# The opening of a hybrid encoder layer on one core: every engine's order written out, and the input projection fed with normed rows only

## Chip, core and metric

The kernel runs on one core of a Trainium2 chip. Time is the device time of one execution, in microseconds (us); smaller is better. TensorE (PE) multiplies, ScalarE (ACT) and VectorE (DVE) work elementwise, GpSimd (POOL) fills and adds, SyncE (SP) issues most loads. Weights of a product are loaded in a row of their own (PEld).

## What is computed

One layer over 528 rows (16 meta tokens and 512 inputs) of width 1024. The rows are normed, one wide projection feeds a recurrent head group (RWKV-7), an attention head group with a forget gate (FoX) and two gates; their results are merged and projected, and an MLP follows.

```python
u = rmsnorm(h, norm_mix[l])
proj = u @ w_in[l]
feat_rw = proj[..., :C_RW]
feat_fx = proj[..., C_RW:C_RW + C_FX]
gates = jax.nn.sigmoid((proj[..., C_RW + C_FX:] + b_gate[l]).astype(jnp.float32))
...
h = h + (merged @ w_o[l]).astype(h.dtype)
z = rmsnorm(h, norm_mlp[l])
h = h + (jnp.square(jax.nn.relu(z @ w_up[l])) @ w_down[l]).astype(h.dtype)
```

The time shift `f + mu * (token_shift(f) - f)` is laid on the RWKV features; `log_f = log_sigmoid(fl + b_f)`, summed up along the rows, gives the forget rows F of the eight attention heads.

## The kernel before

All operands stand transposed: 128 features of a block on the partitions, rows along the free side, in two halves of 264 rows (t = 0, 1). A float32 operand is split into a rounded part and a remainder (`hi`, `lo`), and a product of two such operands is three fast products (`passes`). The rows are split into `uhi` and `ulo`, eight blocks of 128 features each, in four chunks of two; each block of 128 output features of `w_in` is 24 products per half (8 blocks, 3 passes). Plain float32 products take two passes, each at half the pace.

The opening, before the loops over heads, does this. The input comes in four chunks per half (`xt`). For each half, ScalarE squares a chunk (L352), rounds it times the norm's gain to `uhi` (L355), VectorE makes the remainder `ulo` (L356): rows that are **not yet scaled** by the inverse root. TensorE sums the squares with a matrix of ones (L360, `pss`), makes the forget gate's eight columns from the raw rows (L365, `pf`, 24 products per half), and ScalarE takes the inverse root with a logarithm and an exponential (L368, L369, `rs`). The first two blocks of `w_in` (LORA and GD, the low-rank inputs of the decay and of the output gate) are projected from the raw rows in `proj` (L304), and their results are rescaled by `rs` in `normed_shift` (L377) before the time shift (L317, L318). Behind them the forget rows are finished (L381 to L388), and `xt` is scaled, rounded and split anew (L398, L400, L401), which overwrites `uhi` and `ulo` with normed rows for all other blocks.

From there a planner (`Turns`, with the estimate `Clock`) decides while the program is written in which order streams go on: projections of further blocks (L501, with weights rounded at L470 and L471), the first head pair's decay (L733 to L743) and keys (L750 to L769), its score products (L804), attention. A block's weights arrive in two halves (`wraw`, four buffers, one load each on SyncE). Inside the opening a scheduler that follows dependences and readiness orders the engines' queues; every engine then executes its queue in order.

Results of a projection lie in banks: two with the tag `pj`, and one each with `ch` and `py` that the opening may use too. A bank is free again when the time shift has read it.

## Time and profile before

| | us |
|---|---|
| median of 3 runs | 848.71 (846.68 to 849.0) |
| the profiled execution | 847.68 |
| its span, first to last instruction | 845.9 |
| TensorE busy | 827.1 |
| VectorE busy | 615.0 |
| ScalarE busy | 460.4 |
| GpSimd busy | 115.7 |

The profile is one execution. A group of instructions is told by line, engine, operation and tile, with its count, its busy time and the mean of one; the time that an engine stood before an instruction is in brackets, with what released it. The end of a product is modelled, so that products overlap in the rows: the pace is read from the starts.

### The profile page before, as it was taken

The page shows a single profiled execution, that of the slowest core. Times are in us where ns is not written, and L with a number is a line of the kernel's source. Part 1 is how long each engine was busy: PE and PEld are TensorE (multiplying, and loading weights), DVE is VectorE, ACT ScalarE, POOL GpSimd, SP SyncE. Part 2 cuts the span into 40 slices and gives each one's busy share as a digit, 9 for nine tenths or more (in the row PEclk, how much of TensorE's full clock was granted, in tenths as well). Part 3 has the DMA queues.
Part 4 walks back from the last instruction along what each step waited for, and adds up shares of the span by engine and source line. Part 5 has one row for each costly group of instructions (what it writes and reads, how often), then busy time and mean ns, then how long its engine had stood idle before and what let it go on. Part 6 is the DMA issues. An engine that isn't in the chain of part 4 may idle for free.

```text
span 845.9 us, 15282 instructions
## 1 busy us (share of the span) xinstructions
PE 827.1 (98%) x5740; PEld 679.4 (80%) x5740; DVE 615.0 (73%) x1226; ACT 460.4 (54%) x947; POOL 115.7 (14%) x121
## 2 busy tenths in 40 slices
PE   7899999999999999999999999999999999999998
PEld 6888976878988777787688779888888888888886
DVE  7996986589879757566456564876777777767688
ACT  7767537774765276554555452664355435544452
POOL 1010200001000000000022002204700550055000
PEclk9999999999999999999999999999999999999999
DMA  6132131201213222123487422642743374246321
GB/s 229 59 103 66 65 101 42 77 27 64 63 59 95 87 76 77 39 87 101 151 264 228 149 81 88 208 141 56 256 137 100 95 240 128 86 137 200 110 91 74
DMA packets 51338, 95.88 MB, mean 113 GB/s; under 512 B 5816, under 2 KB 6968, under 8 KB 51264
## 3 DMA queue, kind: packets, MB, share of 16 engines
q1 hardware_dynamic: 47680, 86.52, 32.4%
q0 software_dynamic: 1280, 4.20, 1.6%
q10 hardware_dynamic: 2304, 4.20, 1.4%
q8 instruction: 45, 0.74, 0.4%
q14 instruction: 29, 0.24, 0.1%
HBM read 88.57 MB, written 6.31 MB: 112 GB/s over the span
## 4 chain that ended last, share of the span: by engine, by line
PE 76%; DVE 8%; ACT 4%; DMA 4%; issue 2%; POOL 1%; SPq 0%; DVEq 0%; ACTq 0%; POOLq 0%
PE pj L501 21%; PE po L1149 21%; PE po L1267 12%; PE pd L1267 5%; PE po L1119 2%; PE pw L857 2%; DMA gl<-gd 2%; PE psc L611 1%; PE py L656 1%; DMA wraw<-in_wo 1%; PE ppt L640 1%; DVE wlo L236 1%; PE pch L923 1%; PE psr L804 1%; DMA wraw<-in_wup 1%
## 5 line engine op out<-in xcount | busy, mean ns | idle before, releaser
L501 PE MATMUL pj<-uhi,whi 128*128 128x264 f32 (+1 forms) x480 | 166.0, 346 | 0.0
L501 PE MATMUL pj<-ulo,whi 128*128 128x264 f32 (+1 forms) x480 | 154.1, 321 | 1.2 <-DVE ulo L401 1.2
L501 PE MATMUL pj<-uhi,wlo 128*128 128x264 f32 (+1 forms) x480 | 154.0, 321 | 0.0
L501 PEld LDWEIGHTS pj<-uhi,whi 128*128 128x128 f32 x480 | 90.3, 188 | 14.6 <-issue 6.6
L236 DVE TENSOR_TENSOR wlo<-wraw,whi 128x512 fp32r<-128x512 f32 x88 | 67.1, 771 | 46.9 <-ACT whi L235 46.9
L501 PEld LDWEIGHTS pj<-ulo,whi 128*128 128x128 f32 x480 | 90.5, 188 | 8.1 <-issue 1.7
L501 PEld LDWEIGHTS pj<-uhi,wlo 128*128 128x128 f32 x480 | 90.3, 188 | 7.0
L1149 PE MATMUL po<-zhi,whi 128*128 128x512 f32 (+1 forms) x248 | 94.8, 382 | 0.0
L1149 PE MATMUL po<-zlo,whi 128*128 128x512 f32 (+1 forms) x248 | 94.8, 382 | 0.0
L1149 PE MATMUL po<-zhi,wlo 128*128 128x512 f32 (+1 forms) x248 | 94.8, 382 | 0.0
L235 ACT CAST whi<-wraw 128x512 fp32r<-128x512 f32 x88 | 54.0, 618 | 51.9 <-DMA wraw<-in_wup 21.5
L470 ACT CAST whi<-wraw 128x512 fp32r<-128x512 f32 x80 | 48.8, 616 | 38.8 <-PE pj L501 37.9
L471 DVE TENSOR_TENSOR wlo<-wraw,whi 128x512 fp32r<-128x512 f32 x80 | 57.2, 723 | 13.1 <-ACT whi L470 11.3
L270 ACT CAST whi<-t 128x512 fp32r<-128x512 f32 x64 | 39.9, 624 | 44.5 <-DVE wlo L271 20.6
L271 DVE TENSOR_TENSOR wlo<-t,whi 128x512 fp32r<-128x512 f32 x64 | 49.4, 784 | 18.9 <-ACT whi L270 18.0
L1267 PE MATMUL po<-wlo,fhi 128*128 128x512 f32 x160 | 62.7, 392 | 0.2 <-DVE wlo L271 0.2
L1267 PE MATMUL po<-whi,flo 128*128 128x512 f32 x160 | 62.3, 389 | 0.0
L1267 PE MATMUL po<-whi,fhi 128*128 128x512 f32 x160 | 61.9, 389 | 0.0
L1195 POOL TENSOR_TENSOR t<-traw 128x512 f32<-128x512 f32 x24 | 35.4, 1482 | 152.4 <-DVE wlo L271 136.8
L1149 PEld LDWEIGHTS po<-zhi,wlo 128*128 128x128 f32 x248 | 46.6, 188 | 9.1
L1149 PEld LDWEIGHTS po<-zhi,whi 128*128 128x128 f32 x248 | 46.6, 188 | 9.0
L1149 PEld LDWEIGHTS po<-zlo,whi 128*128 128x128 f32 x248 | 46.6, 188 | 8.9
(307 smaller groups left out, 1751.5 us busy)
## 6 DMA issues: line engine op xcount, KB each, us to landing
wraw<-in_win SPq DMA_DIRECT2D x84, 256.0 KB, 2.6
wraw<-in_wup SPq DMA_DIRECT2D x64, 256.0 KB, 3.2
wraw<-in_wdn SPq DMA_DIRECT2D x48, 256.0 KB, 2.6
traw<-in_wdn SPq DMA_DIRECT2D x48, 256.0 KB, 3.0
gd<-gt ACTq DMA_DIRECT2D x16, 256.0 KB, 2.3
wraw<-in_wout SPq DMA_DIRECT2D x16, 256.0 KB, 2.8
gl<-gd SPq DMA_DIRECT2D x16, 256.0 KB, 3.0
wraw<-in_wo SPq DMA_DIRECT2D x16, 256.0 KB, 3.2
```

Source lines behind the costliest of these rows:

```text
L235: A.copy(hi, raw)
L236: low.tensor_tensor(lo, raw, hi.bitcast(F32), ALU.subtract)
L270: A.copy(hi, x)
L271: V.tensor_tensor(lo, x, hi.bitcast(F32), ALU.subtract)
L470: A.copy(hi, raw)
L471: low.tensor_tensor(lo, raw, hi.bitcast(F32), ALU.subtract)
L501: mm(po, a, b[:, k, a0:a1], start=n == 0, stop=n == 23)
L857: mm(ps_[hs, n - b0, :], lhs(n)[hs], rhs(n)[hs], start=True, stop=True)
L1119: mm(po, a[:, k, 128 * i:128 * i + 128], b[:, k, :], start=n == 0, stop=n == 23)
L1149: mm(po[:, t0:t1], a, b[:, k, t0:t1], start=n == 0, stop=n == 23)
L1195: eng.tensor_tensor(t, sums[c, pair] if c in (T1, T2) else c, d, ALU.add)
L1267: mm(x[i], a[:, k, left, 128 * i:128 * i + 128], c, start=start and k == 0 and n == 0, stop=stop and k == n_pairs - 1 and n == 2)
```

## The change

- The opening of TensorE, ScalarE, VectorE and GpSimd is written out by hand (`manual_schedule`): these queues have the order of the code.
- `uhi` and `ulo` are made once, from rows that are already scaled (`scaled`, `upper`, `lower`); the raw split, its 16 roundings and 16 remainders, and the four rescalings of results are gone.
- All squares and gate products stand ahead: half 0's sums with ones are wide as before (L405), half 1's are products with 32 columns of ones, and the gate's with 32 columns of weights (zero beyond the eighth), each in one of four places of the array (`group`, L365). The four parts of half 1's sums are copied and added by one more product with ones (L435, L438), those of the gate by a picking matrix (L458, L469).
- Eight products of ones with ones (`warm`) stand ahead of everything on TensorE.
- LORA and GD are projected together, chunk by chunk (`products`, L390), each half's four chunks in turn. A third block, the first pair's first RWKV block, has its weights loaded and rounded in the opening (`primed`).
- The forget rows (`forget`) are finished behind the first pair's decay; attention waits for them (`forgot`). Tanh goes through a helper that keeps table loads in order, and one tanh of a single column is made ahead.
- Weight loads: LORA, GD, then half 1's chunks, then the third block. Some tiles change their buffers.

```diff
+            raws = []
+            for blk in (B_LORA, B_GD, B_PAIR + 3):
+                if blk == B_PAIR + 3:
+                    for c in range(4):
+                        nc.sync.dma_start(xt[1][:, 2 * c:2 * c + 2, :].rearrange("p a b -> p (a b)"), ht[1, c])
+                for j in range(2):
+                    raw = wp.tile([128, 512], F32, name="wraw", bufs=4)
+                    nc.sync.dma_start(raw, win[blk][:, 512 * j:512 * j + 512])
+                    raws.append(raw)
...
+            def square(t, c):
+                sqs[t, c] = sq = xp.tile([128, 2, HT], F32, name="sq", bufs=4)
+                act(sq, xt[t][:, chunks[c], :], AF.Square)
+            def group(po, c, k, a, b):
+                g = 2 * (c % 2) + k
+                mm(po[32 * g:32 * g + 32], a, b, start=c < 2, stop=c > 1)
+            def gate(t, c):
+                for k in range(2):
+                    group(col[t][1], c, k, wf[:, 2 * c + k, :], xt[t][:, 2 * c + k, :])
+            def root(t):
+                act(rss[t], col[t][0], AF.Ln, bias=eps, scale=1.0 / 1024 / (1, 32)[t])
+                act(rss[t], rss[t], AF.Exp, scale=-0.5)
+            def scaled(t, c):
+                for k in range(2 * c, 2 * c + 2):
+                    V.scalar_tensor_tensor(xt[t][:, k, :], xt[t][:, k, :], pr[:, C_GN + k:C_GN + k + 1], rss[t], ALU.mult, ALU.mult)
...
+            def products(t, c):
+                for q, po in enumerate(pos[t]):
+                    for k in range(2 * c, 2 * c + 2):
+                        i = 2 * q + k // 4
+                        for n, (a, b) in enumerate(passes((ohi[i], olo[i]), U)):
+                            mm(po, a[:, 128 * (k % 4):128 * (k % 4) + 128], b[:, k, tks[t]], start=k + n == 0, stop=k == 7 and n == 2)
...
+            with tc.manual_schedule(engines={ET.PE, ET.Activation, ET.DVE, ET.Pool}):
...
+                warm = psm("warm")
+                for i in range(8):
+                    mm(warm[:, :128], ones, ones, start=True, stop=True)
+                col = [[psm(name)[:, :HT] for name in ("pss", "pf")] for t in range(2)]
+                pos = [[ppj(tag)[:, :HT] for tag in tags] for tags in (("pj", "pj"), ("ch", "py"))]
                 for c in range(4):
-                    sq = xp.tile([128, 2, HT], F32, name="sq", bufs=3)
-                    act(sq, xt[t][:, 2 * c:2 * c + 2, :], AF.Square)
-                    for k in range(2 * c, 2 * c + 2):
-                        gn = pr[:, C_GN + k:C_GN + k + 1]
-                        act(uhi[:, k, tk], xt[t][:, k, :], AF.Copy, scale=gn)
-                        V.scalar_tensor_tensor(ulo[:, k, tk], xt[t][:, k, :], gn, uhi[:, k, tk].bitcast(F32), ALU.mult, ALU.subtract)
+                    square(0, c)
+                    for k in range(2):
+                        mm(col[0][0], ones, sqs[0, c][:, k, :], start=c + k == 0, stop=c + k == 4)
+                    gate(0, c)
+                high(0)
+                rest(0)
+                root(0)
+                scaled(0, 0)
+                high(2)
+                rest(2)
+                upper(0, 0)
+                scaled(0, 1)
+                for c in range(4):
+                    square(1, c)
+                    gate(1, c)
+                    for k in range(2):
+                        group(col[1][0], c, k, ones[:, :32], sqs[1, c][:, k, :])
                     if c == 0:
-                        pq = psm("pss")[:, :HT]
-                    for k in range(2):
-                        mm(pq, ones, sq[:, k, :], start=c + k == 0, stop=c + k == 4)
...
-                rs = xp.tile([128, HT], F32, name="rs")
-                act(rs, pq, AF.Ln, bias=eps, scale=1.0 / 1024)
-                act(rs, rs, AF.Exp, scale=-0.5)
...
-                def normed_shift(po, sl):
-                    V.tensor_tensor(po, po, rss[sl.start // HT], ALU.mult)
-                    shift(po, sl)
-                proj(B_LORA, normed_shift, ((tk.start, tk.stop),), w_lora)
...
+                        lower(0, 0)
+                        high(1)
+                        upper(0, 1)
+                    if c == 1:
+                        scaled(0, 2)
+                        lower(0, 1)
+                        rest(1)
+                        high(3)
+                    if c == 2:
+                        products(0, 0)
+                        upper(0, 2)
+                        rest(3)
+                        scaled(0, 3)
+                        lower(0, 2)
+                A.copy(part[0], col[1][0])
+                col[1][0] = psm("pss")[:, :HT]
+                products(0, 1)
+                mm(col[1][0], ones, part[0], start=True, stop=True)
+                root(1)
+                upper(0, 3)
+                lower(0, 3)
+                products(0, 2)
+                products(0, 3)
+                high(4)
+                tanh(tiny, eps)
+                rest(4)
+                scaled(1, 0)
+                upper(1, 0)
+                shifts[0](pos[0][0], tks[0])
+                scaled(1, 1)
+                lower(1, 0)
+                upper(1, 1)
+                shifts[1](pos[0][1], tks[0])
+                high(5)
+                for c in range(4):
+                    products(1, c)
+                    if c < 2:
+                        A.copy(part[1 + c], col[c][1])
+                        scaled(1, c + 2)
+                        last["ACT"] = upper(1, c + 2)
+                    if c < 3:
+                        lower(1, c + 1)
+                    if c == 1:
+                        rest(5)
+                last["DVE"] = shifts[0](pos[1][0], tks[1])
+                V.tensor_reduce(pick, ident.rearrange("p (g a) -> p a g", g=4)[:, :8, :], AX.X, ALU.add)
+                for t in range(2):
+                    pf = psm("pf")[:8, :HT]
+                    mm(pf, pick, part[1 + t], start=True, stop=True)
+                    V.tensor_tensor(f0[:, tks[t]], pf, rss[t][:8], ALU.mult)
+                shifts[1](pos[1][1], tks[1])
...
+        def forget():
+            s_ = act(f0, f0, AF.Identity, bias=pr[:8, C_BF:C_BF + 1])
+            V.scalar_tensor_tensor(f1, f0, -1.0, f0, ALU.mult, ALU.max)
+            pin = pinned(s_)
+            after(act(f1, f1, AF.Exp, scale=-1.0), pin)
+            after(act(f1, f1, AF.Ln, bias=1.0), pin)
+            V.scalar_tensor_tensor(f1, f0, 0.0, f1, ALU.min, ALU.subtract)
+            V.memset(f0, 1.0)
+            V.tensor_tensor_scan(fF, f0, f1, 0.0, ALU.mult, ALU.subtract)
+            nc.sync.dma_start(fF_d, fF)
+            forgot.done = True
...
             yield from pairs[0].decay()
+            forget()
```

How the order moves, at three places. TensorE, the end of half 0's sums and what follows; before (`pss` are sums of squares, `pf` gate products, `xt0` and `xt1` the halves, `whi` and `wlo` the rounded weights of LORA and their remainder):

```order
L365 MATMUL pf_189<-uhi_96,wf1_153 8x264
L365 MATMUL pf_189<-uhi_96,wf0_152 8x264
L365 MATMUL pf_189<-ulo_97,wf0_152 8x264
L365 MATMUL pf_189<-uhi_96,wf1_153 8x264
L304 MATMUL pj_221<-uhi_96,whi_125 128x264
L304 MATMUL pj_221<-ulo_97,whi_125 128x264
L304 MATMUL pj_221<-uhi_96,wlo_126 128x264
L304 MATMUL pj_221<-uhi_96,whi_125 128x264
```

and now (`ohi0` is the first weight half of LORA):

```order
L365 MATMUL pf_179<-xt0_117,wf_153 32x264 x2
L405 MATMUL pss_178<-sq_204,ones_115 128x264 x2
L365 MATMUL pf_179<-xt0_117,wf_153 32x264 x2
L365 MATMUL pf_181<-xt1_118,wf_153 32x264 x2
L365 MATMUL pss_180<-sq_221,ones_115 32x264 x2
L365 MATMUL pf_181<-xt1_118,wf_153 32x264 x2
L365 MATMUL pss_180<-sq_230,ones_115 32x264 x2
L365 MATMUL pf_181<-xt1_118,wf_153 32x264 x2
L365 MATMUL pss_180<-sq_241,ones_115 32x264 x2
L390 MATMUL pj_182<-uhi_96,ohi0_141 128x264
L390 MATMUL pj_182<-ulo_97,ohi0_141 128x264
```

Before, products of raw rows follow the gate of half 0; now the gate and three of the four sums of half 1 stand ahead of the first product.

ScalarE, from half 0's last squares to its root and behind it; before:

```order
L352 ACTIVATE sq_181<-xt0_116 128x528
L355 ACTIVATE uhi_96<-xt0_116,pr_64 128x264 x2
L352 ACTIVATE sq_249<-xt1_117 128x528
L368 ACTIVATE rs_214<-pss_162,eps_68 128x264
L355 ACTIVATE uhi_96<-xt1_117,pr_64 128x264
L369 ACTIVATE rs_214<-rs_214 128x264
L355 ACTIVATE uhi_96<-xt1_117,pr_64 128x264
L235 CAST whi_141<-wraw_139 128x512
L235 CAST whi_147<-wraw_145 128x512
L352 ACTIVATE sq_258<-xt1_117 128x528
L355 ACTIVATE uhi_96<-xt1_117,pr_64 128x264
```

and now (`ohi1` to `ohi3` are rounded weights, `part0` half 1's partial sums):

```order
L361 ACTIVATE sq_221<-xt1_118 128x528
L354 CAST ohi1_142<-wraw_126 128x512
L380 CAST uhi_96<-xt0_117 128x2x264
L361 ACTIVATE sq_230<-xt1_118 128x528
L354 CAST ohi3_144<-wraw_130 128x512
L361 ACTIVATE sq_241<-xt1_118 128x528
L380 CAST uhi_96<-xt0_117 128x2x264
L361 ACTIVATE sq_264<-xt1_118 128x528
L435 COPY part0_159<-pss_180 128x264
L372 ACTIVATE rs_163<-pss_271,eps_68 128x264
L373 ACTIVATE rs_163<-rs_163 128x264
L380 CAST uhi_96<-xt0_117 128x2x264
```

The squares of half 1 stood among roundings of raw rows; now each stands behind a weight half or a rounding of scaled rows of half 0, and the last rounding of half 0 behind half 1's root.

VectorE, the forget rows (`f0`, `f1`, `fF`); before:

```order
L382 SCALAR_TENSOR_TENSOR f1_108<-f0_107 8x528
L398 SCALAR_TENSOR_TENSOR xt1_117<-xt1_117,pr_64,rs_307 128x264
L471 TENSOR_TENSOR wlo_488<-wraw_483,whi_487 128x512
L377 TENSOR_TENSOR pj_311<-pj_311,rs_307 128x264
L471 TENSOR_TENSOR wlo_492<-wraw_485,whi_491 128x512
L385 SCALAR_TENSOR_TENSOR f1_108<-f0_107,f1_108 8x528
L318 SCALAR_TENSOR_TENSOR lf0_109<-pj_311,pr1_65,tm_219 128x264
L386 MEMSET f0_107 8x528
L314 MEMSET tm_350 128x1
L377 TENSOR_TENSOR pj_352<-pj_352,rs_214 128x264
L387 SCALAR_TENSOR_TENSOR fF_105<-f0_107,f1_108 8x528
```

and now, among the first pair's keys and rows:

```order
L850 SCALAR_TENSOR_TENSOR okk_462<-okk_462,pr_64,sq_573 128x528
L606 SCALAR_TENSOR_TENSOR f1_109<-f0_108,f1_109 8x528
L864 SCALAR_TENSOR_TENSOR L0_662<-okk_462,P_559 128x9x63
L865 TENSOR_SCALAR L0_662<-okk_462 128x9
L855 SCALAR_TENSOR_TENSOR KT_621<-okk_462,lc_557 128x9x64
L607 MEMSET f0_108 8x528
L856 SCALAR_TENSOR_TENSOR BK_620<-tha_443,KT_621 128x9x64
L608 SCALAR_TENSOR_TENSOR fF_106<-f0_108,f1_109 8x528
L858 TENSOR_TENSOR KT_621<-BK_620,P_559 128x1152
L304 SCALAR_TENSOR_TENSOR orr_532<-pj_575,pr1_65,tm_534 128x264
L304 SCALAR_TENSOR_TENSOR orr_532<-pj_602,pr1_65,tm_534 128x264
```

The subtraction, the fill and the scan moved from among half 1's scalings and the rescalings of results to ahead of the first pair's `KT` and the shift of its `orr` block.

## Rows read from the trace of the kernel before

**Rows 1.** The page, first part: busy time, share of the span, instructions.

```profile
PE 827.1 (98%) x5740; PEld 679.4 (80%) x5740; DVE 615.0 (73%) x1226; ACT 460.4 (54%) x947; POOL 115.7 (14%) x121
```

**Rows 2.** Stretches: length, busy (count) of PE, PEld, DVE, ACT, POOL, clock, DMA, GB/s.

```profile
4.77:30.00 25.23, 25.23 (x164) 21.77 (x165) 22.55 (x52) 20.49 (x43) 0.00 (x0) 1.00 0.52 180
30.00:60.00 30.00, 26.61 (x235) 23.90 (x234) 27.50 (x54) 22.56 (x46) 4.45 (x9) 1.00 0.29 91
60.00:100.00 40.00, 39.67 (x354) 34.65 (x352) 31.69 (x57) 27.17 (x57) 6.63 (x7) 1.00 0.18 59
```

**Rows 3.** Groups on TensorE until 60 us: count, busy us, mean ns, idle before.

```profile
L501 PE MATMUL pj<-uhi,whi 128*128 128x264 f32 x48 | 14.0, 291 | 0.0
...
L360 PE MATMUL pss<-sq,ones 128*128 128x264 f32 x32 | 9.8, 464 | 4.8 <-ACT sq L352 4.8
L304 PE MATMUL pj<-uhi,wlo 128*128 128x264 f32 x32 | 9.1, 284 | 0.0
...
L365 PE MATMUL pf<-uhi,wf 128*8 128x264 f32 x32 | 6.8, 301 | 0.0
```

**Rows 4.** Timeline of TensorE: start us, us, line, operation, tile, count.

```profile
9.32 0.48 PE L365 MATMUL pf<-uhi,wf 128*8 128x264 f32 x1
...
9.63 0.29 PE L365 MATMUL pf<-ulo,wf 128*8 128x264 f32 x1
...
10.23 1.13 PE L360 MATMUL pss<-sq,ones 128*128 128x264 f32 x4
...
13.36 0.28 PE L304 MATMUL pj<-uhi,whi 128*128 128x264 f32 x1
...
13.84 0.28 PE L304 MATMUL pj<-ulo,whi 128*128 128x264 f32 x1
...
93.69 0.89 PE L804 MATMUL psr<-L,BK 64*64 64x128 f32 x24
```

**Rows 5.** Sums of squares (pss) alone: length, PE, PEld, ACT, clock, DMA, GB/s.

```profile
5.00:8.40 3.40, 3.40 (x8) 2.63 (x9) 0.00 (x0) 1.00 1.00 337
16.30:19.70 3.40, 3.40 (x16) 2.80 (x16) 0.00 (x0) 1.00 0.41 142
```

**Rows 6.** Timeline, around 40 us; in brackets the wait and its releaser.

```profile
39.40 0.30 ACT L270 CAST lw<-lraw 128x128 fp32r<-128x128 f32 x1 [1.37 <-DMA lraw<-in_lora]
...
40.01 0.70 DVE L401 TENSOR_TENSOR ulo<-xt,uhi 128x528 fp32r<-128x528 f32 x1
...
40.77 0.39 PE L501 MATMUL pj<-ulo,whi 128*128 128x264 f32 x1 [0.95 <-DVE ulo L401]
```

**Rows 7.** Timeline, steps of ScalarE and VectorE in the opening.

```profile
11.41 0.48 ACT L368 ACTIVATE rs<-pss,eps 128x264 f32<-128x264 f32 x1
...
12.19 0.41 ACT L369 ACTIVATE rs<-rs 128x264 f32<-128x264 f32 x1
...
19.10 4.12 DVE L398 SCALAR_TENSOR_TENSOR xt<-xt,pr,rs 128x264 f32<-128x264 f32 x10
...
27.39 1.69 ACT L400 CAST uhi<-xt 128x528 fp32r<-128x528 f32 x3
...
29.10 1.28 ACT L390 ACT_TABLE_LOAD   x1
...
30.36 1.91 DVE L401 TENSOR_TENSOR ulo<-xt,uhi 128x528 fp32r<-128x528 f32 x3
```

**Rows 8.** Timeline, the forget rows on VectorE.

```profile
24.70 0.69 DVE L382 SCALAR_TENSOR_TENSOR f<-f 8x528 f32<-8x528 f32 x1
...
29.20 1.24 DVE L387 TENSOR_TENSOR_SCAN fF<-f,f 8x528 f32<-8x528 f32 x1
```

**Rows 9.** Two stretches (length, PE, clock, DMA, GB/s) and a product in the first.

```profile
415.00:418.40 3.40, 1.72 (x7) 1.00 0.32 54
418.40:421.80 3.40, 3.27 (x8) 0.50 1.00 372
...
417.80 0.49 PE L1070 MATMUL po<-yhi,whi 128*128 128x512 f32 x1 [1.58 <-ACT yhi L270]
```

More of the change, by code (lines that the diff above doesn't have):

```diff
@@ L423 @@
         G.memset(Tt, 0.0)
-        ck = Clock(nc)
+        ck.read()
         turns = Turns(tc, ck)
@@ L693, in load_lora @@
             lw = [wp.tile([128, 128], F32R, name=f"lw{part}{i}", bufs=bufs) for i in range(2)]
-            split(lw[0], lw[1], raw)
+            after(A.copy(lw[0], raw), last["ACT"])
+            V.tensor_tensor(lw[1], raw, lw[0].bitcast(F32), ALU.subtract)
             fetch_lora()
```

111 lines of the change are left out of this document (46 added, 65 removed).

## Prediction, made before the changed kernel ran

> **What bounds the kernel now.** I read the page's first part, then the stretches, then the waits. TensorE is busy for 98% of the span [rows 1]; with so little slack, a change moves the end only by TensorE's own work or by time in which it waits. The stretches show where it waits: 4.77 to 30 us looks full, 30 to 60 has 26.61 of 30.00, and 60 to 100 is full again [rows 2]. (A third stretch, from the start to 4.77, is the wait for the first squares [rows 3].) So the opening is the place, and a lag that is made before 60 us is carried to the end, since nothing behind it has slack to take it up.
>
> "Busy" hides gaps, because one product lasts 0.28 us but the next starts 0.12 after it [rows 4]. So I count work instead. Until 60 us there are 288 products of 264 columns in the split number form: 96 of L304 and 144 of L501 in three groups each, of which one is shown, and 48 of L365, 32 in the row shown. At 0.12 each (four in 13.36 to 13.84) they are 34.6 us. Then 32 passes of L360, two to a product, at 0.22 (16 touch a stretch of 3.40 us, the outer ones in part), 7.0; and about 5.5 of smaller groups, an estimate from the same paces [rows 3 to 5]. That is 47.1 us of work in the 55.2 us since 4.77: **8.1 us are lost**. 2.0 of them are the first nine passes at half rate: 8 passes stand in 3.40 us there, 16 in as much time later [rows 5]. The granted clock reads 1.00 in both rows, so I go by the pace: the lower level, 1.2 instead of 2.4 GHz, in an engine that had done nothing before. The rest are waits for remainders that VectorE rewrites (the last ends at 40.71, TensorE stands 0.95 us for one of them), and a loading chain in which ScalarE stands 1.37 us for a 64 KB load queued behind the two forget-row loads [rows 6].
>
> **Part by part.** The sum is made against the profiled execution, 847.7 us (span 845.9); the median of the runs shown is 848.7, so I add the difference to that.
>
> *TensorE's work.* Removed: 16 wide sums, 7.0 us, and 48 gate products at 0.12, 5.8. Added: 9 wide sums at 0.44, 4.0 us; 24 narrow ones (16 gate, 8 sums, 32 columns of weights), and two wide-rate picks, 0.9. No row shows 32-column products in different places abreast. Nearest rows: 24 quarter-array passes of 128 columns take 0.89 us, 0.037 each [rows 4], where a full-width pass of 264 takes 0.22, 128 columns 0.11; that is about three abreast, four without the last one's tail; the old gate's narrow products, all in one place, go one after the other at 0.12 [rows 3]. Abreast, the order on TensorE makes nine rounds of 0.44, 4.0 us; one by one 10.6; four at once always 2.6. The new ones stand in different places, as the quarter passes do, so I take 4.0. Net **-3.9 us** (-5.3 to +2.7). The 96 opening products stay. The eight warming products run while the first load is on its way.
>
> *Switching between wide and narrow arrays.* The first narrow product after wide ones is followed 0.31 us later instead of 0.12, and the four passes on the way back take 1.13, some 0.08 more than four at 0.22 with the last one's 0.39 in full [rows 4]. The new order goes there and back six times: **+1.7**. The Trainium skill (TensorEngine Tiling (Array Packing), Key Properties) says that different tiles work in parallel but that a change of tiling mode drains the engine; the first half is my nine rounds, which no run here shows, the second agrees with the 0.31 and speaks against this order, which mixes both kinds. By the first half alone the step would be worth -3.9, by both -2.2.
>
> *Half 0 until its scale.* The eight warming products take 16 passes of 128 columns, at half rate about 0.21 each (0.44 for 264), from 1.5 to 5.0 us. Then each chunk costs 0.88 for its sums, 0.44 for the gate and 0.28 for switching: 1.6, three times, plus 0.88, gives 10.7. Logarithm and exponential (0.48, 0.42) end at 11.6 [rows 7]; before, they end at 12.60. Part of this still runs at the lower clock: **0.9** (0 to 1.7; before 2.0).
>
> *Half 1's squares.* They are only four of ScalarE's steps, but they now stand behind half 0's rows, and TensorE's order puts the sums of half 1 ahead of the first products. VectorE scales 264 columns in 0.41 (ten in 4.12 [rows 7]) and needs two of them for a chunk, so chunk 0 is ready at 12.5; ScalarE rounds it (0.56, three in 1.69) and only then squares half 1's chunk 0, done at 13.75. TensorE has been without work since about 11.2: 2.6 us lost. The next squares stand behind another weight half and another rounding each, 15.35 and 16.45: 1.1 and 0.6 more. Together **4.3**. Before, TensorE ran products with raw rows in this time, which need no scale: that was the cover, and it is gone.
>
> *Half 0's end.* Products of chunks 0 and 1 (12 at 0.12 each), the last sums and the folding sum end at 21.4; half 1's scale at 22.5. The rounding of half 0's last chunk stands behind it on ScalarE, 23.1, its remainder 23.9 (0.64 [rows 7]). TensorE has finished chunk 2 at 22.8: **1.0** lost.
>
> *Half 1's start.* Remainder, weight remainder, two scalings: 25.3; the rounding, behind a table load of 1.28 us [rows 7], 26.0; a bank that the first shift must free, 26.9; a remainder at 30.8. Each ends a wait: 0.8, 0.8, 0.7. The pick's products wait 0.7 for what VectorE has ahead of them. **3.0** together. The last remainder of the normed rows then ends near 33.7, seven microseconds before the old 40.71, because 16 roundings and 16 remainders of raw rows and four rescalings of results are gone from ScalarE and VectorE. These are gains only as far as TensorE waited for them, and that is in the 8.1.
>
> *The forget rows.* Their steps move from 24.7 to 30.4 us [rows 8], where TensorE had raw products, to among the first pair's decay and keys. There a subtraction (0.69, as L382), a fill and the scan (1.24) stand ahead of KT and of the evacuation of the r block. VectorE is busy 27.5 of 30 us already between 30 and 60 [rows 2]. Queued behind them are two evacuations and a weight remainder; TensorE waits for the bank they free, about 2.4 us, and for the remainder, 0.6. **3.0** (0 to 3.5), near 56 us. On SyncE's queue the forget rows now stand behind the small loads, so ScalarE's 1.37 us goes; it is in the 8.1.
>
> *The clock.* At 415 to 418.4 TensorE was busy 1.72 of 3.40 us, with one gap of 1.58; in 418.4 to 421.8 the granted clock is 0.50, the level of 1.2 GHz, and 8 products fill 3.27 us where 7 had taken 1.72 [rows 9]. At half rate that stretch cost some 1.7 us. In the new opening TensorE has about 1.8 us of work between 11.2 and 16.9, a smaller share than there. I expect one such fall, on the path to half 1's scale: **+1.7** (0 to 3.4). The Trainium skill (TensorE: Matmul & The Clock Gate, HAM oscillation — how this bites in real kernels) asks for a longer idle gap than any here before the clock falls; by it the fall is absent. The gap of 1.58 in the trace speaks against it.
>
> Sum: -3.9 - 8.1 + 1.7 + 0.9 + 4.3 + 1.0 + 3.0 + 3.0 + 1.7 = +3.6 us. 847.7 becomes 851.3; from the median, **852.3**.
>
> **Rivals.**
> *The clock holds and the start is quick.* The 1.7 and part of the 0.9 go: 850.0 (848 to 851.2). For it: there TensorE had stood 1.58 us at a time, and two of the three new gaps (1.1, 0.6) are shorter; against it: the new gaps add up to more. Chance 0.30.
> *The early rows pay.* Everything from 33.7 us on has its rows seven microseconds sooner. If VectorE gets through the first pair's keys before TensorE runs out of ready blocks, the 3.0 near 56 us vanishes, and with the clock at its higher level and a quick start (1.7 and 0.9) the sum is -2.0: 846.7. The point that decides is whether the r block's evacuation ends before TensorE has used up the blocks at hand, some 2.4 us sooner than my count. For it: VectorE, busy 22.55 of 25.23 us before 30 [rows 2], loses a good part of that load. Against: from 46 us on it is the fuller engine, with the forget rows on top. Chance 0.12.
> *Narrow products one by one.* 6.6 us more work, of which about half falls into the waits for squares: 855.6. For it: no row shows them abreast; against: quarter passes are. Chance 0.13.
> *My forecast*, 851.3 to 854.5: 0.45.
>
> **How the numbers follow.** The range leaves out a tenth on each side: below 848.0 lies most of the second rival, above 857.0 the third with two falls of the clock. A measurement of this kernel tells about 0.3% from no change, 2.5 us. Slower by more than that: 0.45 and 0.13, 0.58; within it 0.30; faster 0.12.
>
> **What would show it.** The profile after should have: the last normed remainder near 34 us; TensorE idle 2 to 3 us before the second half's sums, released by ScalarE's squares; products of chunk 3 waiting on VectorE; a granted clock of 0.50 somewhere before 22 us; idle time on a block of L573 between 54 and 58 us, released by VectorE; nothing new after 100 us. Wrong would be shown by a first product of L390 well before 16 us, by full slices from 10 to 30, or by narrow sums a full 0.44 apart from each other.

## Result and the profile after

The changed kernel takes 851.51 us (median of 6 runs, 850.86 to 853.67) against 847.36 for the kernel before (6 runs beside it): ratio 1.0049, 95% interval 1.0038 to 1.0060. It is slower by more than the 0.3% that a measurement tells from no change. The profiled execution spans 849.8 us, 3.9 more than before.

The first part of the page, the row of busy times, which answers [rows 1]: TensorE is busy for 4.7 us more, VectorE, ScalarE and GpSimd for less.

```profile
PE 831.8 (98%) x5746; PEld 679.4 (80%) x5746; DVE 607.2 (71%) x1208; ACT 455.4 (54%) x934; POOL 114.7 (13%) x121
```

The stretches of [rows 2], and five smaller ones inside them (length, busy time and count of PE, PEld, DVE, ACT and POOL, granted clock, DMA share, GB/s):

```profile
4.77:30.00 25.23, 20.32 (x118) 12.49 (x117) 10.31 (x21) 13.96 (x26) 0.00 (x0) 0.86 0.49 167
30.00:60.00 30.00, 27.58 (x213) 25.71 (x213) 25.58 (x53) 22.54 (x46) 2.15 (x6) 0.99 0.17 54
60.00:100.00 40.00, 39.21 (x366) 32.76 (x365) 32.11 (x62) 25.15 (x53) 6.42 (x8) 0.96 0.32 95
...
11.20:14.40 3.20, 0.68 (x9) 0.16 (x8) 2.10 (x5) 2.59 (x6) 0.00 (x0) 1.00 0.34 131
14.40:16.00 1.60, 0.65 (x8) 0.16 (x8) 1.60 (x5) 1.60 (x5) 0.00 (x0) 0.78 0.50 142
16.00:22.30 6.30, 6.26 (x32) 3.65 (x32) 3.28 (x7) 2.11 (x4) 0.00 (x0) 0.52 0.49 159
...
57.30:59.50 2.20, 0.23 (x2) 0.04 (x2) 2.20 (x4) 0.62 (x1) 0.00 (x0) 1.00 0.04 8
59.50:63.40 3.90, 3.90 (x9) 2.49 (x9) 3.90 (x9) 1.52 (x3) 3.14 (x3) 0.56 0.55 152
```

VectorE is relieved before 30 us, as the diff suggests: 10.31 us busy instead of 22.55. TensorE profits nothing from it: it stands for 4.9 us of that stretch, and from 16.0 to 22.3 it is "full" with 32 passes because it runs at half its clock. In this execution the same happens once more behind a wait at 57 us. TensorE's waits until 110 us (line, what it waited for, sum, times, longest):

```profile
PE pss L365 <- ACT sq L361: 3.5, 2, 2.6
PE pj L573 <- DVE orr L304: 2.0, 1, 2.0
...
PE pj L390 <- DVE ulo L383: 0.7, 2, 0.4
PE pj L573 <- DVE lf L304: 0.5, 1, 0.5
...
PE pj L390 <- ACT uhi L380: 0.5, 1, 0.5
```

And its timeline at the two places (start, duration, line, tile, count, wait and releaser):

```profile
14.46 0.42 PE L365 MATMUL pss<-sq,ones 128*32 128x264 f32 x2 [2.58 <-ACT sq L361]
14.47 0.42 PE L365 MATMUL pf<-xt,wf 128*32 128x264 f32 x2
14.70 0.39 PE L365 MATMUL pss<-sq,ones 128*32 128x264 f32 x2
...
18.12 0.59 PE L390 MATMUL pj<-uhi,ohi 128*128 128x264 f32 x1
18.50 0.42 PE L390 MATMUL pj<-ulo,ohi 128*128 128x264 f32 x1
18.73 0.42 PE L390 MATMUL pj<-uhi,olo 128*128 128x264 f32 x1
...
57.24 0.28 PE L573 MATMUL pj<-uhi,wlo 128*128 128x264 f32 x1
59.50 0.63 PE L573 MATMUL pj<-uhi,whi 128*128 128x512 f32 x1 [1.98 <-DVE orr L304]
59.93 0.63 PE L573 MATMUL pj<-ulo,whi 128*128 128x512 f32 x1
```

Products of 264 columns start 0.22 apart there instead of 0.12, those of 512 columns 0.43 apart, where the same line has 0.23 in other stretches. On VectorE, what stood ahead of the r block's evacuation (`orr`, L304) at that time:

```profile
53.28 0.69 DVE L606 SCALAR_TENSOR_TENSOR f<-f,f 8x528 f32<-8x528 f32 x1
...
55.43 0.50 DVE L607 MEMSET f<- 8x528 f32 x1
55.86 0.68 DVE L856 SCALAR_TENSOR_TENSOR BK<-tha,KT 128x576 f32<-128x576 f32 x1
56.47 1.23 DVE L608 TENSOR_TENSOR_SCAN fF<-f,f 8x528 f32<-8x528 f32 x1
57.63 1.32 DVE L858 TENSOR_TENSOR KT<-BK,P 128x1152 f32<-128x1152 f32 x1
58.88 0.87 DVE L304 SCALAR_TENSOR_TENSOR orr<-pj,pr,tm 128x264 f32<-128x264 f32 x2
```

**Where the 3.9 us come from.** I counted, in both traces, the work that TensorE still has ahead of it at each moment (every group at its own pace), and compared the times at which equal work is left. The changed kernel is then 6.0 us late at 36 us; 2.4 at 52, because the kernel before loses 2.8 us in five waits between 31 and 46 us (0.31 and 0.58 for the low-rank rows, 0.29 and 0.95 [rows 6] for remainders, 0.68 for the keys' squares) and some more in small gaps; 5.5 at 62, behind the second wait and its half clock; 5.3 at 460; and 3.9 from 500 on. From the first product of the MLP to the end both take 326.8 us.

### The profile page after: what moved, and what is told of

Read it like the earlier page. It is cut to its first block, busy times and chain, and to the rows that moved or that the text cites. A ratio compares the mean times of both kernels' runs of the same rounds, so it can differ in the third digit from the quotient of the medians.

```text
span 849.8 us, 15250 instructions
## 1 busy us (share of the span) xinstructions
PE 831.8 (98%) x5746; PEld 679.4 (80%) x5746; DVE 607.2 (71%) x1208; ACT 455.4 (54%) x934; POOL 114.7 (13%) x121
## 4 chain that ended last, share of the span: by engine, by line
PE 83%; DVE 6%; ACT 4%; DMA 3%; issue 2%; POOL 0%; DVEq 0%; SPq 0%; ACTq 0%; POOLq 0%
PE pj L573 24%; PE po L1239 21%; PE po L1357 12%; PE pd L1357 5%; DMA wraw<-in_wo 2%; PE po L1209 2%; PE pw L946 2%; PE po L1160 1%; PE psc L699 1%; PE py L744 1%; PE pj L390 1%; PE ppt L728 1%; DMA gl<-gd 1%; PE psr L893 1%; PE pch L1012 1%
## 5 line engine op out<-in xcount | busy, mean ns | idle before, releaser
L573 PE MATMUL pj<-uhi,whi 128*128 128x264 f32 (+1 forms) x480 | 167.2, 348 | 2.5 <-DVE orr L304 2.0
L573 PE MATMUL pj<-uhi,wlo 128*128 128x264 f32 (+1 forms) x480 | 154.8, 322 | 0.0
L573 PE MATMUL pj<-ulo,whi 128*128 128x264 f32 (+1 forms) x480 | 154.6, 322 | 0.0
L573 PEld LDWEIGHTS pj<-uhi,whi 128*128 128x128 f32 x480 | 90.5, 189 | 17.4 <-issue 8.1
L573 PEld LDWEIGHTS pj<-uhi,wlo 128*128 128x128 f32 x480 | 90.7, 189 | 8.1 <-DVE wlo L543 0.6
L236 DVE TENSOR_TENSOR wlo<-wraw,whi 128x512 fp32r<-128x512 f32 x84 | 66.1, 795 | 42.5 <-ACT whi L235 42.3
L573 PEld LDWEIGHTS pj<-ulo,whi 128*128 128x128 f32 x480 | 90.8, 189 | 6.9 <-issue 1.9
L235 ACT CAST whi<-wraw 128x512 fp32r<-128x512 f32 x84 | 51.6, 617 | 54.6 <-DMA wraw<-in_wup 24.2
L542 ACT CAST whi<-wraw 128x512 fp32r<-128x512 f32 x78 | 47.8, 617 | 44.8 <-PE pj L573 44.2
L543 DVE TENSOR_TENSOR wlo<-wraw,whi 128x512 fp32r<-128x512 f32 x78 | 53.2, 690 | 14.6 <-ACT whi L542 14.2
L1285 POOL TENSOR_TENSOR t<-traw 128x512 f32<-128x512 f32 x24 | 34.6, 1447 | 153.9 <-DVE wlo L271 136.9
```

What stands on the lines that cost most here:

```text
L235: A.copy(hi, raw)
L236: low.tensor_tensor(lo, raw, hi.bitcast(F32), ALU.subtract)
L542: after(A.copy(hi, raw), last["ACT"])
L543: after(V.tensor_tensor(lo, raw, hi.bitcast(F32), ALU.subtract), last["DVE"])
L573: mm(po, a, b[:, k, a0:a1], start=n == 0, stop=n == 23)
L1285: eng.tensor_tensor(t, sums[c, pair] if c in (T1, T2) else c, d, ALU.add)
```

## Experiments

Every kernel below was timed beside the kernel before. The landmarks are read from one trace each: where VectorE's last remainder of the normed rows ends, when the first product of the output projection starts (`po<-yhi`, L1070 or its like), how long it is from there to the first product of the MLP, and the span.

| kernel | last remainder | output projection | from there to MLP | span | ratio to before (95%) |
|---|---|---|---|---|---|
| before | 40.7 | 417.8 | 101.2 | 845.9 | 1 |
| after | 36.6 | 423.0 | 100.0 | 849.8 | 1.0049 (1.0038 to 1.0060) |
| e1 forget rows in the opening | 36.6 | 434.0 | 100.5 | 861.3 | 1.0181 (1.0168 to 1.0194) |
| e2 filler in the waits | 35.1 | 420.5 | 100.5 | 847.9 | 1.0035 (1.0021 to 1.0049) |
| e3 squares first | 35.9 | 421.4 | 99.6 | 848.1 | 1.0036 (1.0022 to 1.0049) |
| e4 before, forget rows moved | 43.5 | 423.3 | 101.3 | 852.0 | 1.0045 (1.0032 to 1.0057) |
| e5 forget rows later | 35.7 | 420.8 | 101.2 | 848.9 | 1.0039 (1.0025 to 1.0053) |
| e6 e2 and e5 | 35.2 | 420.2 | 102.0 | 849.0 | 1.0041 (1.0026 to 1.0055) |
| e7 no warming | 38.2 | 423.7 | 102.1 | 852.6 | 1.0076 (1.0061 to 1.0091) |
| e8 wide sums | 34.6 | 421.0 | 101.2 | 849.1 | 1.0044 (1.0029 to 1.0060) |
| e9 reordered | 34.4 | 420.7 | 99.7 | 847.2 | 1.0025 (1.0016 to 1.0033) |
| e10 e9 and e5 | 34.0 | 419.7 | 100.8 | 847.3 | 1.0015 (1.0006 to 1.0024) |
| e11 mended | 29.9 | 416.6 | 99.2 | 842.7 | 0.9977 (0.9968 to 0.9986) |
| e12 e11, forget rows whole | 29.5 | 415.6 | 100.6 | 843.2 | 0.9971 (0.9960 to 0.9982) |

The fourth column is to be kept in mind: the same instructions take 99.2 to 102.1 us there, with waits for `in_wo` loads in different places, and I could find no relation to how early they start. So a gain of 1 to 2 us ahead of 417 us shows in the landmarks of a trace, and hardly in the times; e2 to e6 and e8 are not told apart from the changed kernel by their intervals. One trace says little below 1 us, too: up to 40 us the changed kernel, e1 and e5 are the same code, but their first inverse root ends at 12.26, 13.20 and 12.54, their granted clock from 16.9 to 22 us is 0.50, 0.67 and 0.73, and their last remainder ends at 36.6, 36.6 and 35.7.

**e1, forget rows in the opening.** The whole of `forget` stands behind the opening, ahead of the tanh of LORA.

```diff
+            s_ = act(f0, f0, AF.Identity, bias=pr[:8, C_BF:C_BF + 1])
...
+            V.tensor_tensor_scan(fF, f0, f1, 0.0, ALU.mult, ALU.subtract)
+            nc.sync.dma_start(fF_d, fF)
             tanh(lf[:64], lf[:64])
```

> The changed kernel with the forget rows finished right behind the opening, ahead of the tanh of the LORA block, where VectorE stands idle 1 to 1.5 us at a time. Theory (place in VectorE's queue): the three steps (0.69, 0.50, 1.23 us) no longer stand ahead of the evacuation of the r block, so TensorE's wait of 2.1 us at 57.2 goes, and with it the half clock behind it (9 products at 0.43 instead of 0.23, 1.8 us): about 848.5. Rival (amount, not place): VectorE has no room from 40 to 62 us, the steps push other work back by as much and the same wait turns up at another block: 851.5, within 0.5. Rival (given back): the wait goes, but the kernel had slack for part of it later: 849.5 to 850.5.

It took 863.39 us: neither theory. ScalarE's timeline says why.

```profile
42.01 1.28 ACT L262 ACT_TABLE_LOAD   x1
43.30 0.64 ACT L475 ACTIVATE f<-f 8x528 f32<-8x528 f32 x1
43.97 1.28 ACT L255 ACT_TABLE_LOAD   x1
...
45.93 1.28 ACT L476 ACT_TABLE_LOAD   x1
...
49.29 1.28 ACT L255 ACT_TABLE_LOAD   x1
...
53.02 1.28 ACT L262 ACT_TABLE_LOAD   x1
```

The exponential (L475) and the logarithm (L476) fall between tanh steps, and each change of function loads a table, five times 1.28 us in eleven where the changed kernel has one (47.17). TensorE then waits 3.9 us for a rounded weight. By equal work left, 4.9 of the 11.5 us are there at 100 us, a half clock from 58 to 65 us included. Most of the rest comes between there and the output projection, where the planner laid out another order of the streams; why that order is slower stays open. The Trainium skill (ScalarE activation tables: per-element evaluation and per-set limits, What a function is on this engine) gives 1283 ns for a switch between sets; the rows agree. So the place behind the decay, where that table is loaded anyway, has a reason, and this run says nothing on VectorE's queue. e5 isolates that.

**e2, filler.** Products of ones in the waits for the second half's squares.

```diff
                     gate(1, c)
+                    for i in range((11, 4, 3, 0)[c]):
+                        mm(pos[1][0][:, :128], ones, ones, start=True, stop=True)
```

> The changed kernel with 18 more products of ones on TensorE (11, 4 and 3) in its three waits for the second half's squares; their results are overwritten. Theory (the clock falls because TensorE stands): granted clock 1.00 from 16.9 to 22 us instead of 0.50, the 12 products there 0.12 apart instead of 0.22 and the narrow groups 0.24 a round instead of 0.44: some 2.3 us off, 849.2, though TensorE has more to do. Rival (the slow pace comes from the switching between narrow and wide arrays, or from loads): the pace stays at 0.22, and the added products cost 0 to 0.5: 851.5 to 852.

The stretch of the half clock, and two products in it:

```profile
16.00:22.30 6.30, 6.30 (x53) 4.43 (x52) 3.54 (x7) 2.75 (x6) 0.00 (x0) 1.00 0.52 160
...
18.62 0.28 PE L390 MATMUL pj<-ulo,ohi 128*128 128x264 f32 x1
18.74 0.28 PE L390 MATMUL pj<-uhi,olo 128*128 128x264 f32 x1
```

The clock stays at 1.00 and the pace at 0.12, with no fewer switches and the same loads as in the changed kernel: TensorE's standing is the cause. The last remainder comes 1.5 us sooner (2.3 were expected, the filler overran its waits a little), the output projection 2.5, since the half clock at 59 us is absent too, although the wait for `orr` of 1.99 us is there. The time fell by a seventh of a percent, within both intervals; the traced execution, at 849.7 us, lies near the lower end of ten between 849.0 and 853.2.

**e3, squares first.** The four squares of the second half right behind the first root.

```diff
                 root(0)
+                for c in range(4):
+                    square(1, c)
                 scaled(0, 0)
```

> The changed kernel with ScalarE's four squares of the second half moved up to right behind the inverse root of the first. Theory (TensorE's waits for these squares are on the path): the waits of 2.6, 0.9 and 0.9 us shrink to one of about 1.3, the first product of L390 starts near 16.6 instead of 18.1, and the clock holds in part: 1.5 to 3 us off, 849.2. Rival (ScalarE and VectorE, with the same work as before, set when the second half's rows are ready): TensorE's waits move behind 23 us, the last remainder stays at 36.6, and the time at 851.0 to 851.6.

The wait for squares shrank to 0.97 us, as the theory has it, but the first products then waited 0.93 and 1.23 us for the first half's rounding and remainder, and the last remainder moved by only 0.7 us. The rival was nearer: the work of ScalarE, 5.09 us busy of 5.70 between 11.2 and 16.9 in the changed kernel, and of VectorE, busy for all of the 5.10 us from 16.9 to 22 here, is still ahead of the rows. The 0.7 lies within what traces of one code differ by.

**e4, the forget rows alone.** The kernel before, with `forget` behind the first pair's decay.

```diff
-            act(f0, f0, AF.Identity, bias=pr[:8, C_BF:C_BF + 1])
...
             yield from pairs[0].decay()
+            forget()
```

> The kernel before with this one part of the change: the forget rows finished behind the first pair's decay (in buffers that are free there). Theory (place in VectorE's queue): subtraction, fill and scan stand ahead of the evacuation of the r block, TensorE waits 1 to 2.5 us between 50 and 58 us and may lose as much again to the clock: 849.5 to 851, against 847.4. Rival (the later wait in the changed kernel comes from its later rows, not from the forget rows): within 0.5 us of before; below it, if 24 to 30 us profits.

851.54 us: the size is the theory's, but the place isn't. TensorE stands for a rounding of the last rows, which the scheduler put behind ScalarE's forget steps:

```profile
41.41 0.59 PE L492 MATMUL pj<-uhi,whi 128*128 128x264 f32 x1 [2.90 <-ACT uhi L391]
...
41.50:48.00 6.50, 6.07 (x24) 5.46 (x25) 6.44 (x14) 6.25 (x12) 0.14 (x1) 0.50 0.24 72
```

There, too, a half clock follows the wait, and together they are the loss in this trace, whose execution (853.81) is the longest of five. This run shows that the forget rows cost as much as the whole change when they are laid among the first pair's steps; it doesn't show that VectorE's queue is how.

**e5, only VectorE's three steps later.** `forget` is cut in two; subtraction, fill and scan follow the first pair's scores.

```diff
+        def forget_end(prev):
+            after(V.scalar_tensor_tensor(f1, f0, 0.0, f1, ALU.min, ALU.subtract), prev)
+            after(V.memset(f0, 1.0), prev)
...
                     yield from q.scores()
+                    if g == 0 and j == 0:
+                        forget_end(q.masked)
```

> The changed kernel; ScalarE's steps of the forget rows stay where they are, only VectorE's last three (subtraction, fill, scan: 0.69, 0.50, 1.23 us) move behind the first pair's scores, to about 66 us, long before attention reads the rows (126 us). Theory (place in VectorE's queue, from which the earlier move into the opening did not isolate them, since it added table loads on ScalarE): the wait of 2.0 us for the r block's evacuation at 57 us shrinks below 0.5, the half clock behind it (1.0 us after other losses) goes: 3 us off, 848.5. Rival (VectorE is full from 53 to 66 us, whatever stands there): the wait turns up again at the scores, and the time stays within 0.7 of 851.5.

The wait for `orr` is gone, and a shorter one for the next weight remainder stands nearly in its place:

```profile
58.12 0.50 PE L573 MATMUL pj<-uhi,wlo 128*128 128x512 f32 x1 [1.14 <-DVE wlo L543]
```

No half clock follows (1.00 from 54 to 66 us). By equal work left, the kernel is 1.0 us ahead of the changed one at 56 (the first half clock was shorter in this execution, 0.73 against 0.50 from 16.9 to 22), 3.2 at 66 and 2.2 at 80: so the place costs 1.3 to 2.2 us with the half clock that follows in the changed kernel's trace, and in the new place VectorE being full costs another 1.1. Both theories hold a part.

**e6, e2 and e5 together.**

> Both at once: 18 products of ones in the waits for the second half's squares, and VectorE's three steps of the forget rows behind the first pair's scores. If the two losses are independent: 1.5 us from the opening and 3 from 57 us, 847.0, level with before (847.4 to 848.1). Rival (the half clock at 58 to 62 us was shared: the filler alone already made it vanish there, in its profile): 848 to 848.5. If the forget rows' place costs nothing: 849.9.

850.96 us, no case's number. In the trace it is 2.8 us ahead of the changed kernel at the output projection, little more than e2's 2.5, as the first rival has it, and 0.8 in the span, since this execution took 102.0 us to the MLP. The times don't tell it apart from e2 or e5. That the filler is what took the half clock at 59 us away is not shown: e3, e7 and e9 have no filler, the same wait of 2.0 us for `orr`, and no half clock behind it either.

**e7, one warming product instead of eight** (`range(1)` for `range(8)`).

> The changed kernel with one warming product of ones instead of eight. Theory (they bring the clock up while the first chunk is loaded): the first four wide sums and the gate products behind them run at half rate (0.44 a pass instead of 0.22) until about 9 us, the first half's inverse root ends 1 to 2 us later than 12.3 and everything behind it: 852.5 to 853.5. Rival (the loads of chunks 2 and 3, which land at 6.1 and 7.6 us, set the pace until then): under 0.4 us, 851.5 to 851.9.

The first four passes of wide sums, at half rate, and, below, four at full rate later in the same trace:

```profile
4.69 2.13 PE L405 MATMUL pss<-sq,ones 128*128 128x264 f32 x4 [2.38 <-ACT sq L361]
...
10.36 1.16 PE L405 MATMUL pss<-sq,ones 128*128 128x264 f32 x4
```

In the changed kernel the first four take 1.16 us as well. The first root ends at 14.14 us, against 12.05 to 13.20 in the eleven traces with eight warming products; in e1 and e3, among these, the first four passes still run at half rate (1.96 and 1.90 us up to the gate's, against 1.09). Everything behind is 1.6 us later than in the changed kernel until 60 us, and the time is 0.27% above: the theory holds for the opening. Of the 2.8 us in the span, though, 0.7 are left at the output projection, with no half clock at 59 us, and 2.1 come from there to the MLP; how much of the 0.27% is the warming stays open.

**e8, wide sums in the second half**, without places, copy and folding product.

```diff
-                        group(col[1][0], c, k, ones[:, :32], sqs[1, c][:, k, :])
+                        mm(col[1][0], ones, sqs[1, c][:, k, :], start=c + k == 0, stop=c + k == 4)
...
-                mm(col[1][0], ones, part[0], start=True, stop=True)
```

> The changed kernel with the second half's sums of squares as wide products, as in the first half (0.44 each instead of a place beside the gate products); the folding product and ScalarE's copy ahead of it go. Theory (the narrow sums save work that is on the path, as the sum of the prediction counts it): eight wide sums, 3.5 us, take the place of places in groups that run for the gate anyway, and 0.7 of folding go; some of it falls into the waits for squares: 1 to 2 us more, 852.5 to 853.5. Rival (TensorE waits there anyway, and more work holds the clock up): 850 to 851.5.

The rival: 851.54 us, and in the trace 2.0 us ahead of the changed kernel from 27 us to 460. Two stretches of it:

```profile
16.90:22.00 5.10, 5.10 (x30) 3.55 (x31) 3.05 (x6) 1.88 (x4) 0.00 (x0) 1.00 0.54 176
...
58.00:62.00 4.00, 3.94 (x28) 2.73 (x31) 3.80 (x8) 1.18 (x3) 2.85 (x3) 0.60 0.71 191
```

With more work TensorE keeps its full clock from 16.9 to 22 us, although the wait of 2.58 us ahead of it is the same; copy and folding product are gone as well, and the run doesn't part their share from the clock's. Behind the wait at 57 us the clock falls here as in the changed kernel. The narrow sums save work where TensorE stands anyway.

**e9, another order.** Built on e8: ScalarE and VectorE make all four weight halves ahead of the first root, where they stand (2.45 and 2.69 us); then square and rounding in turn.

```diff
+for i in range(4):
+    high(i)
+    rest(i)
+root(0)
+square(1, 0)
+scaled(0, 0)
+half1(0)
+upper(0, 0)
...
```

> The changed kernel with its opening in another order: ScalarE's roundings and VectorE's remainders of all four weight halves ahead of the first inverse root, where both engines stand (2.45 and 2.69 us); behind it, square of the second half and rounding of the first in turn; wide sums in the second half as in the wide-sums run. Theory (ScalarE, 5.1 us busy of 5.7 between 11.2 and 16.9, sets when TensorE gets its rows): four steps of 0.6 less there, so the first product of L390 at about 15 us instead of 18.1, no half clock, the second half's inverse root near 19.5 instead of 25.7, and at 36 us some 3 to 4 us less lag than in the changed kernel: 848 to 849. Rival (from 20 us on VectorE sets the pace with a scaling and a remainder for each chunk, 0.89 and 0.70, against 1.45 of products): waits move to the second half's chunks, and only about the 2.0 us of the wide-sums run are kept: 850.5.

The first product of L390 starts at 15.5 instead of 18.1, and at 24 us the kernel is 3.7 us ahead; at 36 only 1.6 are left. What took them is in the rows (TensorE, then ScalarE):

```profile
29.01 0.39 PE L570 MATMUL pj<-uhi,whi 128*128 128x264 f32 x1 [2.02 <-DVE lf L304]
...
26.56 1.28 ACT L255 ACT_TABLE_LOAD   x1
...
27.96 0.84 ACT L303 ACTIVATE tm<-pj,pr 128x264 f32<-128x264 f32 x2
```

The third block needs a bank that the first block's time shift has to free, and that stands behind a table load. Its price is the wait and, again, a half clock. Behind the wait for `orr`, as long as in the changed kernel, none follows:

```profile
29.00:33.00 4.00, 3.99 (x20) 3.99 (x21) 3.30 (x7) 1.50 (x4) 0.00 (x0) 0.59 0.00 0
...
PE pj L570 <- DVE orr L304: 2.0, 1, 2.0
...
58.00:62.00 4.00, 3.80 (x37) 2.57 (x37) 4.00 (x9) 1.56 (x4) 3.14 (x3) 1.00 0.63 181
```

**e10, e9 and e5.**

> The same, with VectorE's three steps of the forget rows behind the first pair's scores. Theory (two independent losses): 1 to 2 us below the reordered opening alone, 846.5 to 847.5, at or below the kernel before (847.8). Rival (what is gained ahead of 460 us is taken back where the weights of in_wo are loaded, as 0.6 to 2 us were in the runs so far): 848.5 to 849.5.

848.87 us, 0.1% below e9 by the ratios: nearer the rival. In this pair, where the clock holds behind 57 us in both traces, the output projection starts 1.0 us sooner, of which 0.4 are there at the last remainder: without a fall of the clock the place of the three steps costs 0.6 to 1.0 us.

**e11, mended.** Built on e10: the third block's weight halves ahead of the second root, one chunk scaled ahead of each remainder, the time shifts ahead of the table load.

```diff
 products(0, 1)
+high(4)
+rest(4)
+high(5)
+rest(5)
 root(1)
 scaled(1, 0)
...
 products(0, 3)
+shifts[0](pos[0][0], tks[0])
...
 A.copy(part[1], col[0][1])
 tanh(tiny, eps)
```

> The reordered opening with the forget rows behind the scores, mended where its own trace showed waits: the two halves of the third block's weight are rounded ahead of the second half's inverse root, while ScalarE and VectorE stand; behind the root VectorE scales one chunk ahead of each remainder; the time shift that frees the third block's bank goes ahead of the 1.28 us table load for tanh. Theory (the wait of 2.0 us at 26.6 for that bank and the 20 products at half rate behind it, 2.0 us more, come from ScalarE's order alone): neither is there, the last remainder of the second half ends near 29 instead of 34, and the time is 3 to 4 us below the reordered run: 845 to 846, below the kernel before (847.2 to 848.1). Rival (from 40 us on ScalarE and VectorE have no room, so rows that come sooner wait at the first pair's keys): the gain of the opening turns into a longer wait near 55 us, 847.5 to 848.5.

845.27 us against 847.65, 0.23% below the kernel before (0.14 to 0.32): the theory, and a version that beats both kernels. The stretches behind 22 us:

```profile
22.00:30.00 8.00, 8.00 (x66) 7.82 (x65) 6.58 (x15) 4.24 (x9) 0.00 (x0) 1.00 0.01 2
30.00:40.00 10.00, 10.00 (x82) 8.87 (x81) 7.39 (x18) 9.09 (x19) 0.28 (x2) 1.00 0.25 82
...
50.00:54.00 4.00, 2.72 (x20) 2.24 (x19) 4.00 (x6) 2.49 (x5) 3.04 (x2) 1.00 0.02 4
```

From 14 to 52 us no wait of TensorE is in the trace, and at 44 it is 3.3 us ahead of the kernel before, 3.6 ahead of e10. What is left until 60 us is a wait of 1.3 at 52.

**e12, ScalarE's forget steps moved too.**

> The mended opening, with ScalarE's exponential and logarithm of the forget rows moved too: they now stand behind the first pair's rows instead of ahead of its keys' exponential. Theory (with the opening mended, ScalarE is the engine that bounds 40 to 50 us, busy 9.69 of 10, and holds VectorE up for 2.06 us at 45 us): 1.3 us less there, VectorE's wait and TensorE's wait of 1.3 us at 52 shrink to below 0.5, and the time falls by about 1 us: 844.2 against 845.3. Rival (VectorE's own queue up to 53 us is the bound, or what is gained is taken back at the weights of in_wo): within 0.5 of the mended run, 844.8 to 845.8.

845.00 us, within 0.5 of e11. VectorE's wait of 2.06 us and TensorE's of 1.3 at 52 us are gone from the trace, 0.8 is lost at the first scores instead, and the kernel is 1.0 ahead of e11 until 460 us; in its execution the loads of `in_wo` cost 1.3 more. The theory holds for the place, the rival for the time.

## Why the prediction was right, and what in it was not

Forecast were 852.3 us from a median of 848.7, a ratio of 1.0042; measured are 851.5 from 847.4, 1.0049. The signs that it named are in the profile: TensorE idle 2.6 us ahead of the second half's sums, released by ScalarE's squares; a granted clock of 0.50 ahead of 22 us; products of chunk 3 waiting on VectorE (0.36 us for `ulo` at 27.04); a wait at a block of L573, released by VectorE, at 57 us. One sign is off: the last normed remainder ends at 36.6 us, not near 34, for the prediction's dates along the opening left out the half clock, which its sum counts as a term of its own, and the first root came 0.65 late. Term by term:

- *Work, -3.9.* Right. The narrow products run four abreast: at 14.46 and 14.47 two groups of two start, their second passes at 14.70, 0.24 a pass. The Trainium skill (TensorEngine Tiling (Array Packing), Key Properties) says of tiles that they work in parallel; the rows agree. e8 showed, though, that the half of this saving that lies in the second half's sums was worth nothing, since TensorE stands there: a term of work counts only where the work is the bound.
- *Switching, +1.7.* About right: two gate products and the way back take 0.57 us from 6.25 to 6.82, where their two passes need 0.48, and the way in costs 0.2: 0.3 there and back, six times.
- *Half 0 at lower clock, +0.9.* Not in this trace: no sum runs at half rate. But the sums begin 0.16 later, a chunk takes 1.66 instead of 1.6, and the last four passes take 1.16 instead of 0.88, so the first root ends at 12.26 instead of 11.6: 0.65 late by TensorE's own pace. In e1 and e3, with the same warming products, the first four passes do run at half rate, and the root ends another 0.9 later: the term, with its range from 0 to 1.7, holds for some executions and not for others.
- *Waits for half 1's squares, +4.3.* Right as a count: from the starts, at 0.24 a pass, 2.8, 1.1 and 0.6 (the rows have waits of 2.58 and 0.93; passes at half rate fill the third). As a cause it was half a truth. e3 took most of them away and gained 0.7; they are how the load of ScalarE and VectorE shows.
- *Half 0's end, +1.0.* 0.25 and 0.62 before the products of chunk 3: right.
- *Half 1's start, +3.0.* Waits of 0.6, 0.8 and 0.5; the pick's products do not wait. Too much by 1.1.
- *Forget rows, +3.0 near 56 us.* 2.1 at 57.2, no second wait; for the place e5 gives 1.3 to 2.2 with a half clock, e9 against e10 0.6 to 1.0 without.
- *Clock, +1.7 for one fall.* The first fall costs 12 products 0.1 each and the groups beside them some 0.9: 2.1. The second, at 59.5 us, was not forecast: nine products in 3.9 us that take 2.1 at the pace of 0.23, 1.8 more. The prediction priced the wait at the r block with no fall behind it, though the term's range, 0 to 3.4, has room for a second: of the terms for the clock this is the one that came out short. It belongs to this execution rather than to the wait. In six traces TensorE stands 2.0 us for `orr`; the clock falls behind it in the changed kernel and in e8, and holds in e2, e3, e7 and e9. Over the six executions of the changed kernel the mean granted clock is 0.991 in two, the profiled one among them, 0.993 in one and 0.996 in three; by an estimate from these means the three spend some 8 us less at half clock, so not every fall of the profiled one is in them. Their times, 850.9 to 851.5, are at most 0.7 below its 851.5.
- *Old losses, -8.1.* Too much. At 52 us, ahead of the forget rows and of an old loss of 0.84 at 58, the sum has the changed kernel 1.4 us late (3.6 less 3.0, and the 0.84 still to come), and it is 2.4 late. The terms above account for -0.95 of that (+0.65 and +0.4 too low, 0.9 and 1.1 too high), so some 1.9 of the 8.1 were not won back. The waits recorded until 60 us are 3.4 of them and the first passes at half rate 2.0; I take the 1.9 for the small gaps at narrow groups (L822, L469: 0.1 to 0.3 at each of a dozen products), which stand in both kernels. This is worked out, no run shows it.
- *Nothing new after 100 us.* Right until 460; there the stretch with `in_wo` gave 1.3 us back in the profiled pair. What decides how long that stretch takes stays open.

So the sign and the place of each loss came from the rows, and the sum is close because what it had too low (a second fall of the clock, 1.8; too large a credit for old losses, 1.9; 1.05 in the first root and the first fall) met 2.9 that it had too high (0.9 at the root, 1.1 at half 1's start, 0.9 at the forget rows) and the 1.3 given back. That these cancel is luck. The early-rows rival fell as it was argued: the rows come 4 us sooner, and VectorE uses them up at 57 us.

On the clock, the Trainium skill (TensorE: Matmul & The Clock Gate, HAM oscillation — how this bites in real kernels) asks for a longer idle gap than the 2.58 and 1.98 us here. The traces differ: the clock fell to 0.50 behind both, behind 2.90 in e4 and behind 2.02 in e9. It did not fall behind the same 2.58 in e8, where TensorE had more to do around the wait, nor behind 2.0 for `orr` in e2, e3, e7 and e9, where it had the same to do as in the changed kernel: no gap by itself decides it here, and what does stays open.

## What to carry to other kernels

Count a wait of TensorE with a second price: the slower clock that can stand behind it. It cost about as much again at 59 us in the changed kernel, in e4 and in e9, and nothing behind the same wait in e2, e3 and e7, so it is a range and not a figure; a single trace shows one draw of it. Before taking work off an engine, ask which engine hands the next operand over: here the order of ScalarE's and VectorE's steps, not VectorE's total load or TensorE's work, set the opening. Five weight halves on both engines moved into time in which they stood anyway, with wide sums and the forget rows out of the way, turned +0.5% into -0.2%; e9 to e11 moved both engines' steps at once, and no run parts their shares. An order written by hand fixes mistakes as firmly as good choices: the trace of each version names the next one, a bank behind a table load, a fill behind keys.

## What the runs showed of the hardware

36 added passes of products that nobody reads kept the granted clock at 1.00 where it had been 0.52 from 16.0 to 22.3 us, and the last remainder came 1.5 us sooner (e2). The clock is not the same from execution to execution of the same code: from 16.9 to 22 us it is 0.50, 0.67 and 0.73 in the changed kernel, e1 and e5, and behind equal waits of 2.0 us at 57 us it fell in two traces of six. A table load costs ScalarE 1.28 us, and where five of them started within eleven us, TensorE lost 5 us by 100 us, a half clock included (e1). The record of the granted clock reads 1.00 from 4.77 to 8.40 us in e7 too, though the first four passes and the gate's switch take 2.06 us there against 1.09 in the changed kernel: early on, the pace tells the clock and the record doesn't.
